# Grouped-query attention on one core: GpSimd's share of VectorE's exp product sized by the stretch beside which it runs

## The chip, the core and the metric

The kernel runs on one core of a Trainium2 chip. The core has TensorE (PE in the profile, its weight loads PEld), VectorE (DVE), ScalarE (ACT), GpSimd (POOL) and SyncE (SP); each takes its own instructions in order, and DMA queues move data beside them. The metric is the device time of one execution in microseconds (us); the kernel before takes 361.26 us, the median of three runs (361.14 to 361.68).

## What is computed

For 8 batches, 8 query heads and 2 key/value heads, 1024 positions and head size 64, in float32:

```
scores = q @ k.T / sqrt(64)          # 1024 x 1024 for each of the 64 (batch, head)
attn   = exp(scores - max) ; attn = attn / (sum(attn) + 1e-8)
out    = attn @ v                    # query heads 0-3 use key/value head 0, heads 4-7 head 1
```

The kernel leaves out the maximum (the inputs are small) and divides by the sum at the very end, after the product with the values, to which a column of ones is added so that the same matmul gives the sum.

## The kernel before

A "head" below is one of the 64 pairs (batch, query head). The 1024 keys of a head are eight blocks of 128. For one block, TensorE makes the scores with all 1024 queries in one of three PSUM slots `sp0` to `sp2` (two matmuls of 64x512 columns, line 794). Then one of two engines takes the exponential of the 128x1024 scores out of PSUM:

- ScalarE by one ACTIVATE into a buffer `pt` (line 804).
- VectorE by a "chain". One TENSOR_SCALAR from PSUM (`dpass`, line 815) turns the scores into 16-bit numbers `yt` whose bits are exponent and fraction. When two blocks are there, three operations on 128x2048 elements in SBUF follow: `zh` (line 822) makes a second factor from the fraction's bits in `zt`, `two` (line 829) takes the power of two into `et`, and `mul` (line 838) multiplies `yt` into `zt`. The sum of `et` and `zt` is the exponential; TensorE adds them by using both as weights. Only in the last three heads (TAIL) does VectorE add them itself (`add`, line 843).

In the steady part GpSimd takes a part of each `mul`: the last 320 of the 1024 columns of each block of a chain (`GC`, line 57; line 768), so VectorE multiplies 2 x 704 columns. At most two products wait for GpSimd at a time (`GQ`); a chain that finds them waiting multiplies all 2048 columns on VectorE. Which of the blocks go to VectorE is set by a quota: two of the eight blocks of every head, three in every tenth head (`MXD`, `MORE`).

The second matmuls (`pv`, line 856) use blocks of exp as weights and the values as the moving operand, 65 columns each, and fill banks `op0` and `op1` with seven 65-column pieces at a time. When a bank is full VectorE makes seven reciprocals (`rec`, line 921) and multiplies (`norm`, line 930) out of PSUM into `ost`; SyncE's queue stores a head's result (line 934).

GpSimd's queue holds, in one order: the products (line 768), the copies of values into `va`, a tile for all 16 (batch, key/value head) (`place_v`, line 596), and the DMA issues that cast queries and keys to bf16 in DRAM (`cast_q`, `cast_k`, lines 563 to 582). SyncE's queue holds the loads that turn them (lines 604 and 614), copies of the keys, loads of values and the stores.

The order of every queue is written before the kernel is built by a planner (class `Plan`). It keeps a clock for TensorE, ScalarE and VectorE with a duration for each instruction (the `M_` constants), lets ScalarE take its blocks in turn, lets VectorE take, in this order, a waiting `dpass`, a `rec`, or the best of a `norm` and the chains' next steps (`dve`, lines 201 to 277), and at each choice of TensorE tries the alternatives for `HORIZON` ns ahead and keeps the one with the least idle time of ScalarE (weight `W_A`), of VectorE (`W_D`) and lost time of TensorE (`W_P`). A product for GpSimd is put down at the start of a `dpass` (`gpsimd`, lines 188 to 199), so it runs beside it, and it waits for the VectorE instruction ahead of that `dpass` (line 771). PE work that uses a product is planned for `M_GLATE` ns after its end.

The cast DMAs have due times. After the first product each is held until a product is emitted whose successor is over 2300 ns off, and then stands behind that product in GpSimd's queue (lines 773 to 775); one held for over 3000 ns is emitted at the next event, wherever that is (lines 754 and 755). Each waits for the last score matmul emitted before it (line 751).

Of the kernel before, what the change touches and what calls it, by code (L numbers as in the profile page):

```python
# [20 lines left out]
M_SEE = 51  # L21
# [4 lines left out]
M_PVTAIL = 180  # L26
M_ACT = 917
M_ATAIL = 107
M_FIX = 66
# [5 lines left out]
M_REC = 90  # L35
M_GP = 850
M_GLATE = 1500

# [5 lines left out]

HORIZON = 5500
W_A = 1.0
W_D = .28
W_P = .1
W_LAG = 0
# [4 lines left out]
MXD = 2  # L54
MORE = 10
TAIL = 3
GC = 320
GQ = 2
STEPS = (("zh", M_D4), ("two", M_D4), ("mul", M_D2), ("add", M_D2))


class Chain:


    def __init__(self, id, nsteps):
        self.id, self.nsteps = id, nsteps
        self.pairs = []
        self.at = 0
        self.parts = 1
        self.cols = 1024  # L70
        self.end = 0
# [7 lines left out]
    def left(self):  # L79
        n = len(self.pairs)  # L80
        return sum(
            M_FIX + (self.cols if k == "mul" else 1024) * n * r
            for k, r in STEPS[self.at : self.nsteps]
        )


class State:
    LISTS = "nxt dcount pcnt pmax a_of mms slot aq dq out norms lastp firstp twice".split()

    def copy(self):  # L90
        c = State.__new__(State)
        c.__dict__.update(self.__dict__)
        for k in self.LISTS:
            setattr(c, k, getattr(self, k)[:])
        new = {}

        def twin(ch):
            if ch is None:
                return None
# [6 lines left out]
        c.gq = [(t, twin(x), i) for t, x, i in self.gq]  # L106
        c.heads = {k: v[:] for k, v in self.heads.items()}
        c.ev = None
        return c
# [6 lines left out]
class Plan:  # L116
# [5 lines left out]
    def __init__(self, nj, npt, nct, nyt):  # L122
# [7 lines left out]
        self.group_of = [g for g, (lo, hi) in enumerate(self.groups) for _ in range(lo, hi)]  # L130
        self.qready = [M_START] + [M_START + M_Q1 + M_QSTEP * j for j in range(nj - 1)]
        s = State()
        s.nxt = [0] * nj
# [7 lines left out]
        s.out = [M_START, M_START]  # L141
        s.norms, s.gq = [], []
        s.tP = s.tA = M_START
# [43 lines left out]

    def gpsimd(self, s, t, j):

        g = s.placed + 1  # L190
        if 4 * g - 1 <= j < self.nj and 4 * g < self.nj:
            s.placed = g
            s.note(t, "gplace", None, g, None)
            s.tG = t + M_GP
        elif s.gq and s.gq[0][0] <= t and s.tG <= t:
            _, ch, i = s.gq.pop(0)
            s.note(t, "gmul", None, ch.id, i)
            s.tG = t + M_GP
            self.part(s, ch, s.tG + M_SEE + M_GLATE)

    def dve(self, s):
        t, nj, end = s.tD, self.nj, None
        if s.dq and s.dq[0][0] <= t:
            _, sl, j, c = s.dq.pop(0)
# [9 lines left out]
            ch = s.open  # L214
            ch.pairs.append((j, c))
            if j not in s.heads[ch.id]:
                s.heads[ch.id].append(j)
            self.gpsimd(s, t, j)
            s.note(t, "dpass", sl, (ch.id, len(ch.pairs) - 1), (j, c))
            end = t + M_FIX + 1024 * M_D1  # L220
            s.slot[sl] = end + M_DTAIL + M_SEE
            s.dlast = (ch.id, 0)
            if len(ch.pairs) == 2:
                s.chains.append(ch)
                s.open = None
        elif s.norms and s.norms[0][0] <= t and s.norms[0][1] == "rec":
            _, _, lo, hi = s.norms[0]
            s.note(t, "rec", (lo, hi), None, None)
            end = t + M_REC
            s.dlast = lo  # L230
            s.norms[0] = (end, "norm", lo, hi)
        else:
            best = None
            if s.norms and s.norms[0][0] <= t:
                late = s.dlast == s.norms[0][2]
                best = (late, 5 if late else 0, None)
            for ch in s.chains:

                late = s.dlast == (ch.id, ch.at) and ch.at in (0, 3)
                key = (late, 3 - ch.at, ch)  # L240
                if best is None or key[:2] < best[:2]:
                    best = key
            if best:
                at = max(t, s.dend + M_DEP) if best[0] else t
                ch = best[2]
                if ch is None:
                    _, _, lo, hi = s.norms.pop(0)
                    s.note(t, "norm", (lo, hi), None, None)
                    end = at + M_FIX + 64 * (hi - lo) * M_D1
                    s.out[self.group_of[lo] % 2] = end + M_DTAIL + M_SEE  # L250
                    s.dlast = None
                    s.end = s.pc == self.last and not s.left and not s.norms
                else:
                    n = len(ch.pairs)
                    kind, rate = STEPS[ch.at]
                    if kind == "zh" and GC and ch.pairs[0][0] < nj - 5 and len(s.gq) < GQ:
                        end = at + M_FIX + 1024 * n * rate
                        s.gq += [(end + M_DTAIL + M_SEE, ch, i) for i in range(n)]
                        ch.parts += n
                        ch.cols -= GC  # L260
                    cols = ch.cols if kind == "mul" else 1024
                    s.note(t, kind, None, ch.id, n, cols)
                    end = at + M_FIX + cols * n * rate
                    ch.at += 1
                    s.dlast = (ch.id, ch.at)
                    if ch.at == ch.nsteps:
                        s.chains.remove(ch)
                        self.part(s, ch, end + M_DTAIL + M_SEE)
# [4 lines left out]
        else:  # L273
            s.tD = max(t, s.tP) + 1
            for q in (s.dq, s.norms):
                if q:
                    s.tD = min(s.tD, q[0][0])

    def pick_d(self, s):
        for j in range(s.a, min(self.nj, s.a + 3)):  # L280
            if s.nxt[j] < 8 and s.dcount[j] < MXD + (j % MORE == MORE // 2) and self.qready[j] <= s.tP:
                return j
        return None

    def choices(self, s):
# [14 lines left out]
        dj = None  # L300
        held = len({ch.id for ch in s.chains} | {x[1].id for x in s.gq})
        if not s.dq and held < self.nyt and (s.open or s.used_c < self.nct):
# [184 lines left out]
def kernel(  # L487
# [29 lines left out]
    NCT = 8  # L517
    NYT = 4
    plan = Plan(NJ, NPT - 2, NCT - 1, NYT - 1)

# [39 lines left out]
    nc.vector.memset(va[:, :, :, :, D : D + 1], 1.0)  # L560
    kt, qt, qd, kd, vs = {}, {}, {}, {}, {}
# [33 lines left out]
    def place_v(b, g):  # L595
        return nc.gpsimd.tensor_copy(  # L596
            out=va[:, b * G + g, :, :, 0:D],
            in_=vs.pop((b, g)).rearrange("p c (two d) -> p c two d", two=2),
# [130 lines left out]
    def flat(t):  # L729
        return t.bitcast(BF16).rearrange("p i a b -> p i (a b)")  # L730

# [21 lines left out]
    for when, kind, x, j, c, *cols in ev:  # L753
        if casts and casts[0][0] < when - 3000:
            cast(*casts.pop(0)[1:])
        if kind in ("ck", "cq"):

            if gps is None or not GC:
                cast(kind, j)
            else:  # L760
                casts.append((when, kind, j))
        elif kind in ("gmul", "gplace"):
# [3 lines left out]
            else:  # L766
                z = flat(zt[j])[:, c, 1024 - GC :]
                gps = nc.gpsimd.tensor_tensor(  # L768
                    out=z, in0=flat(yt[j])[:, c, 1024 - GC :], in1=z, op=ALU.mult
                )  # L770
# [39 lines left out]
        elif kind == "dpass":  # L810
            ch, i = j
            where[c] = j
            if i == 0:
                yt[ch] = yp.tile([128, 2, 2, HS], U16, name="yt")
            vec = nc.vector.tensor_scalar(  # L815
# [3 lines left out]
        elif kind == "zh":  # L819

            zt[j] = zp.tile([128, 2, 2, HS], U16, name="zt")
            vec = nc.vector.tensor_scalar(  # L822
# [3 lines left out]
        elif kind == "two":  # L826

            et[j] = ep.tile([128, 2, 2, HS], U16, name="et")
            vec = ins = nc.vector.tensor_scalar(  # L829
# [6 lines left out]
        elif kind == "mul":  # L836
            z = flat(zt[j])[:, 0:c, 0 : cols[0]]
            vec = nc.vector.tensor_tensor(  # L838
                out=z, in0=flat(yt[j])[:, 0:c, 0 : cols[0]], in1=z, op=ALU.mult
            )  # L840
# [5 lines left out]
        elif kind == "pv":  # L846
# [7 lines left out]
            for i in range(j, j + c):  # L854
# [10 lines left out]
        elif kind == "pvf":  # L865
# [4 lines left out]
            for i in range(NPIECE):  # L870
# [4 lines left out]
                for n, p in enumerate(every):  # L875
                    nc.tensor.matmul(
                        ops[i // 4][:, lo : lo + D + 1],
                        lhsT=p[:, i // 2 * 128 : (i // 2 + 1) * 128],
                        rhs=va[:, 0, ci % NH, ci // NH, :],
                        start=(first and i % 4 == 0 and n == 0),  # L880
# [3 lines left out]
        elif kind == "pvl":  # L884
# [4 lines left out]
            for i in range(NPIECE):  # L889
# [5 lines left out]
                for n, (ci, p) in enumerate(every):  # L895
                    nc.tensor.matmul(  # L896
                        sps[plan.spare][:, i // 4, lo : lo + D + 1],
                        lhsT=p[:, i // 2 * 128 : (i // 2 + 1) * 128],
                        rhs=va[:, b * G + h // HPG, ci % NH, ci // NH, :],
                        start=(first and i % 4 == 0 and n == 0),  # L900
# [68 lines left out]
```

The softmax here doesn't subtract the row's maximum and nothing guards it: scores larger than these inputs give would overflow.

## Time and profile before

| | us |
|---|---|
| median of three runs | 361.26 |
| lowest and highest | 361.14, 361.68 |
| span of the profiled execution | 359.6 |
| PE busy | 348.5 (97%) |
| DVE busy | 349.7 (97%), 494 instructions |
| ACT busy | 351.1 (98%), 382 instructions, 378 of them exponentials |
| POOL busy | 124.6 (35%) |

The profiled execution's own time is its span; the median of the runs is 1.6 us above it. In the profile a group's line reads: line of the code, engine, operation, output and inputs with their shapes, the number of instructions, then busy time, mean duration of one in ns, and the idle time just before them with what ended it. In the view of instructions in order of time a line starts with the start and the duration in us. An ACT or DVE record ends a little after the next instruction has started, since results are still being written, so durations add up to more than the busy time.

### The profile page before, as it was taken

Reading aid. Unit: us, or ns where it says so; the run is one execution under the profiler, and the core shown is the slowest. Engines: PE = TensorE matmul, PEld = TensorE weight load, DVE = VectorE, ACT = ScalarE, POOL = GpSimd, SP = SyncE. Lnnn points to the kernel's source line nnn. Section 1 sums busy time; section 2 is a strip of 40 time slices with the busy share of each in tenths; the row PEclk is TensorE's granted clock in tenths of the full one; section 3 lists DMA queues with packets and bytes.
Section 4 is the critical chain, followed back from the end, with each engine's and each line's share of the span. In section 5 each row is a group of like instructions: output and inputs, shape, how many; then the busy total and the mean of one; then the engine's idle time right before and its main releaser. Section 6 shows DMA issues by size and latency. Waiting matters only on the chain.

```text
span 359.6 us, 14110 instructions
## 1 busy us (share of the span) xinstructions
PE 348.5 (97%) x6223; PEld 224.1 (62%) x6223; DVE 349.7 (97%) x494; ACT 351.1 (98%) x382; POOL 124.6 (35%) x190
## 2 busy tenths in 40 slices
PE   8889999999999999999999999999999999999995
PEld 4446666666666666666666666666666566666664
DVE  4999999999999999999999999999999999999994
ACT  5999999999999999999999999999999999999995
POOL 4134244344443344242333534144414243321000
PEclk9999999999999999999999999999999999999999
DMA  8634675664697868567557877666477457655132
GB/s 186 114 52 115 138 120 137 132 121 119 132 161 119 148 117 152 113 111 164 120 102 143 128 163 125 132 126 140 107 114 163 105 118 132 154 129 106 46 89 89
DMA packets 89404, 44.82 MB, mean 125 GB/s; under 512 B 46000, under 2 KB 87600, under 8 KB 88112
## 3 DMA queue, kind: packets, MB, share of 16 engines
q1 hardware_dynamic: 86208, 33.44, 41.5%
q0 software_dynamic: 2992, 10.23, 20.4%
q8 instruction: 48, 0.79, 0.9%
q10 hardware_dynamic: 144, 0.26, 0.2%
q14 instruction: 12, 0.10, 0.1%
HBM read 25.17 MB, written 27.00 MB: 145 GB/s over the span
## 4 chain that ended last, share of the span: by engine, by line
DVE 71%; ACT 19%; PE 4%; issue 4%; DMA 1%; DVEq 0%
DVE yt L815 34%; ACT pt L804 19%; DVE zt L838 12%; DVE et L829 8%; DVE ost L930 7%; DVE zt L822 7%; DVE rec L921 2%; PE ops L856 2%; PE sp L794 2%; DMA q<-in_q_dram 1%; PE sp L896 1%; PE sp L673 0%; DVE kt L694 0%; PE ops L685 0%; ACT q L662 0%
## 5 line engine op out<-in xcount | busy, mean ns | idle before, releaser
L804 ACT ACTIVATE pt<-sp 128x1024 bf16<-128x1024 f32 x378 | 348.5, 1051 | 0.7 <-PE sp L794 0.5
L794 PE MATMUL sp<-qt,kt 64*128 64x512 bf16 x1024 | 173.4, 382 | 5.8 <-ACT pt L804 2.7
L856 PE MATMUL ops<-va,pt 128*128 128x65 bf16 x2928 | 176.0, 194 | 0.0
L815 DVE TENSOR_SCALAR yt<-sp 128x1024 uint16<-128x1024 f32 x134 | 162.5, 1213 | 0.5 <-PE sp L794 0.5
L856 PEld LDWEIGHTS <-pt 128*128 128x128 bf16 x2928 | 130.9, 97 | 32.9 <-issue 32.9
L856 PE MATMUL ops<-va,zt 128*128 128x65 bf16 x1040 | 125.7, 194 | 0.0
L856 PE MATMUL ops<-va,et 128*128 128x65 bf16 x1008 | 119.5, 194 | 0.0
L768 POOL TENSOR_TENSOR zt<-yt,zt 128x320 bf16<-128x320 bf16 x90 | 71.0, 789 | 120.1 <-DVE zt L838 32.9
L856 PEld LDWEIGHTS <-et 128*128 128x128 bf16 x1008 | 81.2, 98 | 21.3 <-issue 21.0
L856 PEld LDWEIGHTS <-zt 128*128 128x128 bf16 x1040 | 84.8, 97 | 10.2 <-issue 10.2
L794 PEld LDWEIGHTS <-kt 64*128 64x128 bf16 x1024 | 49.0, 93 | 58.2 <-issue 37.0
L838 DVE TENSOR_TENSOR zt<-yt,zt 128x1408 bf16<-128x1408 bf16 (+1 forms) x67 | 66.2, 989 | 0.0
L571 POOL DMA_DIRECT2D qd<-in_q_dram x62 | 36.0, 581 | 45.0 <-PE sp L794 41.8
L822 DVE TENSOR_SCALAR zt<-yt 128x2048 uint16<-128x2048 uint16 x67 | 46.2, 689 | 0.4
L829 DVE TENSOR_SCALAR et<-yt 128x2048 uint16<-128x2048 uint16 x67 | 45.4, 677 | 0.0
L930 DVE TENSOR_TENSOR ost<-ops,rec 128x448 f32<-128x448 f32 (+2 forms) x73 | 44.4, 608 | 0.4
L596 POOL CAST va<-vs 128x512 bf16<-128x512 f32 x16 | 9.8, 614 | 24.1 <-DVE ost L930 8.8
L921 DVE RECIPROCAL rec<-ops 128x7 f32<-128x7 f32 (+2 forms) x73 | 14.0, 192 | 0.0
L579 POOL DMA_DIRECT2D kd<-in_k_dram x15 | 8.5, 569 | 11.6 <-PE sp L794 11.6
L650 PE MATMUL ops<-warm 128*128 128x128 bf16 (+1 forms) x63 | 9.2, 265 | 1.2 <-DVE warm L559 1.2
L650 PEld LDWEIGHTS <-warm 128*128 128x128 bf16 x63 | 4.4, 104 | 6.7 <-issue 5.5
L843 DVE TENSOR_TENSOR zt<-et,zt 128x2048 bf16<-128x2048 bf16 x3 | 3.7, 1221 | 0.0
(37 smaller groups left out, 24.4 us busy)
## 6 DMA issues: line engine op xcount, KB each, us to landing
out_dram<-ost SPq DMA_DIRECT2D x64, 256.0 KB, 3.1
qd<-in_q_dram POOLq DMA_DIRECT2D x63, 128.0 KB, 3.5
vs<-in_v_dram SPq DMA_DIRECT2D x16, 256.0 KB, 3.3
kd<-in_k_dram POOLq DMA_DIRECT2D x15, 128.0 KB, 3.1
kt<-kt SPq DMA_DIRECT2D x30, 64.0 KB, 2.9
qt<-qd SPq DMA_TRANSPOSE x63, 4.0
q<-in_q_dram ACTq DMA_DIRECT2D x1, 256.0 KB, 3.2
kt<-kd SPq DMA_TRANSPOSE x15, 3.8
```

The lines of the kernel that those rows point to most:

```text
L571: return nc.gpsimd.dma_start(out=t.rearrange("(a x) d -> a (x d)", x=4), in_=q[b, h].rearrange("(a x) d -> a (x d)", x=8),)
L650: nc.tensor.matmul(ops[bank][:, lo : lo + cols], lhsT=warm[:, 0:128], rhs=warm[:, 0:cols], start=not beside, stop=True, skip_group_check=b ...
L768: gps = nc.gpsimd.tensor_tensor(out=z, in0=flat(yt[j])[:, c, 1024 - GC :], in1=z, op=ALU.mult)
L794: now = nc.tensor.matmul(sps[x][:, half, :], lhsT=t[lo : lo + D, c // NH, ci % NH * 128 : (ci % NH + 1) * 128], rhs=qt[j][lo : lo + D, 0, ...
L804: exps.append(nc.scalar.activation(out=p, in_=where_s[(j, c)], func=AF.Exp, scale=scale))
L815: vec = nc.vector.tensor_scalar(out=yt[ch][:, i, :, :], in0=where_s[c], scalar1=EXP_A, scalar2=EXP_B, op0=ALU.mult, op1=ALU.add,)
L822: vec = nc.vector.tensor_scalar(out=zt[j][:, 0:c], in0=yt[j][:, 0:c], scalar1=0x7F, scalar2=0x3F00, op0=ALU.bitwise_and, op1=ALU.bitwise_or,)
L829: vec = ins = nc.vector.tensor_scalar(out=et[j][:, 0:c], in0=yt[j][:, 0:c], scalar1=0x7F80, scalar2=None, op0=ALU.bitwise_and,)
L838: vec = nc.vector.tensor_tensor(out=z, in0=flat(yt[j])[:, 0:c, 0 : cols[0]], in1=z, op=ALU.mult)
L856: nc.tensor.matmul(ops[plan.group_of[x] % 2][:, lo : lo + D + 1], lhsT=p[:, qs * 128 : (qs + 1) * 128], rhs=va[:, b * G + h // HPG, ci % N ...
L921: vec = nc.vector.reciprocal(out=to, in_=sums)
L930: vec = nc.vector.tensor_tensor(out=to, in0=o, in1=by, op=ALU.mult)
```

## The change

The products for GpSimd are no longer a fixed 320 columns of each block. At the start of a `dpass` the planner looks at the stretch in which VectorE will read PSUM: the `dpass` alone (1134 ns), or with a `norm` behind it (531 ns more), or with a `rec` ahead and a `norm` behind. From that it takes away a lead and a fixed cost and divides the rest by 2.09 ns per column; so many columns, in steps of 32, are taken off the end of the two blocks of a chain, seen as 2048 columns in a row. A chain waits with its `mul` for up to two such products (`GWINS`), and VectorE may stay idle for up to 500 ns for a coming `dpass` rather than start that `mul` (`M_SPARE`). When a `norm` is ready it is put right behind the next `dpass` (`follow`). Chains that begin in the first two heads or the last five get no product.

The quota of VectorE is two blocks of a head and three in every fifth head, and 2, 1, 1 in the first three. `va` is four tiles in a ring. Chains' buffers `yt` are six, not four. The planner's ScalarE duration is 923 ns, not 917, `HORIZON` 8000, not 5500, and `W_P` 0; the order of all queues is a new plan.

The instructions of the two kernels, by count: exponentials on ScalarE 378 and 374; `dpass` 134 and 138; `zh` and `two` 67 each and 70 each (two of them of 1024 elements); `mul` 67 (45 of 1408 columns and 22 of 2048) and 70 (21 of 960, 13 of 2048, 13 of 1632, 9 of 1216, 5 each of 1376 and 1248, 2 of 1024, one of 928 and one of 1344); `add` 3, and 3 and one of 1024; products on GpSimd 90 of 320 columns, and 58 of 416, 26 of 672, 5 of 384 and 2 of 704; `rec` and `norm` 74 each in both; the DMAs are the same.

```diff
-M_ACT = 917
+M_ACT = 923
...
-M_GP = 850
-M_GLATE = 1500
+M_GP = 800
+M_GLEAD = 160
+M_GFIX = 120
+M_GCOL = 2.09
+M_GOVER = 60
+M_GLATE = 900
+M_NORM = 531
+M_HOLD = 2500
+M_SPARE = 500
...
-HORIZON = 5500
+HORIZON = 8000
...
-W_P = .1
+W_P = 0
...
-MORE = 10
+MORE = 5
 TAIL = 3
-GC = 320
-GQ = 2
+CHN = 2
+LONG = 6
+FIRST = (2, 1, 1)
+GWINS = 2
+GFROM = 2
+GTO = 5
+GMIN = 192
+GSTEP = 32
...
-        self.cols = 1024
+        self.cols = 0
+        self.wins = 0
+        self.zend = INF
...
+        self.quota = [FIRST[j] if j < len(FIRST) else MXD + (j % MORE == MORE // 2) for j in range(nj)]
...
-    def gpsimd(self, s, t, j):
-
+    def gpsimd(self, s, t, j, window):
+
+
+        at = max(t, s.tG)
+        until = t + window + M_GOVER
+        at += M_GLEAD
         g = s.placed + 1
-        if 4 * g - 1 <= j < self.nj and 4 * g < self.nj:
+        if 4 * g - 1 <= j < self.nj and 4 * g < self.nj and at + 614 <= until:
             s.placed = g
             s.note(t, "gplace", None, g, None)
-            s.tG = t + M_GP
-        elif s.gq and s.gq[0][0] <= t and s.tG <= t:
-            _, ch, i = s.gq.pop(0)
-            s.note(t, "gmul", None, ch.id, i)
-            s.tG = t + M_GP
+            at = s.tG = at + 614
+        for ch in s.chains:
+            if not (ch.zend <= at and 1 <= ch.at <= 2 and ch.nsteps == 3):
+                continue
+            if not GFROM <= ch.pairs[0][0] < self.nj - GTO:
+                continue
+            w = int((until - at - M_GFIX) / M_GCOL) // GSTEP * GSTEP
+            if w < GMIN:
+                break
+            if ch.cols - w < GMIN:
+                w = ch.cols
+            if not w:
+                continue
+            ch.cols -= w
+            ch.wins += 1
+            s.note(t, "gmul", None, ch.id, (ch.cols, w))
+            s.tG = at = at + M_GFIX + w * M_GCOL
+            ch.parts += 1
             self.part(s, ch, s.tG + M_SEE + M_GLATE)
+            break
...
     def dve(self, s):
         t, nj, end = s.tD, self.nj, None
-        if s.dq and s.dq[0][0] <= t:
+        norm = s.norms and s.norms[0][0] <= t
+        rec = norm and s.norms[0][1] == "rec"
+        soon = s.dq and s.dq[0][0] <= t + (M_REC if rec else 0)
+        if rec:
+            _, _, lo, hi = s.norms[0]
+            if soon:
+                self.gpsimd(s, t, s.dq[0][2], M_REC + 1134 + M_NORM)
+                s.host = True
+            s.note(t, "rec", (lo, hi), None, None)
+            end = t + M_REC
+            s.dlast = lo
+            s.norms[0] = (end, "norm", lo, hi)
+        elif s.dq and s.dq[0][0] <= t and not (norm and t - s.norms[0][0] > M_HOLD):
...
+            ch.cols += 1024
             if j not in s.heads[ch.id]:
                 s.heads[ch.id].append(j)
-            self.gpsimd(s, t, j)
+            if not s.host:
+                self.gpsimd(s, t, j, 1134 + (M_NORM if norm else 0))
+            s.host = False
+            s.follow = bool(norm)
...
             best = None
-            if s.norms and s.norms[0][0] <= t:
+            if norm:
                 late = s.dlast == s.norms[0][2]
-                best = (late, 5 if late else 0, None)
+                key = -1 if s.follow or s.norms[0][2] < NPIECE else 5 if late or s.dq else 0
+                best = (late and key >= 0, key, None)
             for ch in s.chains:
 
                 late = s.dlast == (ch.id, ch.at) and ch.at in (0, 3)
-                key = (late, 3 - ch.at, ch)
+                first = (3, 4, 2, 1)[ch.at]
+                if ch.at == 2 and ch.nsteps == 3 and ch.cols and ch.wins < GWINS:
+                    if GFROM <= ch.pairs[0][0] < nj - GTO:
+                        if s.dq and s.dq[0][0] < t + M_SPARE:
+                            continue
+                        first = 6
+                key = (late, first, ch)
                 if best is None or key[:2] < best[:2]:
                     best = key
+            s.follow = False
...
                     kind, rate = STEPS[ch.at]
-                    if kind == "zh" and GC and ch.pairs[0][0] < nj - 5 and len(s.gq) < GQ:
-                        end = at + M_FIX + 1024 * n * rate
-                        s.gq += [(end + M_DTAIL + M_SEE, ch, i) for i in range(n)]
-                        ch.parts += n
-                        ch.cols -= GC
-                    cols = ch.cols if kind == "mul" else 1024
-                    s.note(t, kind, None, ch.id, n, cols)
-                    end = at + M_FIX + cols * n * rate
+                    cols = ch.cols if kind == "mul" else 1024 * n
+                    end = at
+                    if cols:
+                        s.note(t, kind, None, ch.id, n, cols)
+                        end = at + M_FIX + cols * rate
+                    if kind == "zh":
+                        ch.zend = end + M_DTAIL + M_SEE
...
-    NYT = 4
-    plan = Plan(NJ, NPT - 2, NCT - 1, NYT - 1)
+    NYT = 6
+    NVA = 4
+    plan = Plan(NJ, NPT - 2, NCT - 1, NYT - 2)
...
-    va = kvp.tile([128, B * G, NH, 2, D + 1], BF16, name="va")
+    va = [kvp.tile([128, NH, 2, D + 1], BF16, name=f"va{i}") for i in range(NVA)]
...
-                z = flat(zt[j])[:, c, 1024 - GC :]
+                lo, w = c
+                z = flat(zt[j])[:, lo : lo + w]
                 gps = nc.gpsimd.tensor_tensor(
-                    out=z, in0=flat(yt[j])[:, c, 1024 - GC :], in1=z, op=ALU.mult
+                    out=z, in0=flat(yt[j])[:, lo : lo + w], in1=z, op=ALU.mult
                 )
...
-                    rhs=va[:, b * G + h // HPG, ci % NH, ci // NH, :],
+                    rhs=va[(b * G + h // HPG) % NVA][:, ci % NH, ci // NH, :],
```

More of the change, by code (lines that the diff above doesn't have):

```diff
@@ L81, in left, with share @@
         return sum(
-            M_FIX + (self.cols if k == "mul" else 1024) * n * r
+            M_FIX + (self.share() if k == "mul" else 1024 * n) * r
             for k, r in STEPS[self.at : self.nsteps]
         )
+    def share(self):
+        return max(0, self.cols - 500 * max(0, GWINS - self.wins)) if self.nsteps == 3 else self.cols
 class State:
@@ L105, in copy @@
         c.open = twin(self.open)
-        c.gq = [(t, twin(x), i) for t, x, i in self.gq]
         c.heads = {k: v[:] for k, v in self.heads.items()}
@@ L141, in __init__ @@
         s.out = [M_START, M_START]
-        s.norms, s.gq = [], []
+        s.norms = []
+        s.host = s.follow = False
         s.tP = s.tA = M_START
@@ L222, in dve @@
             s.dlast = (ch.id, 0)
-            if len(ch.pairs) == 2:
+            if len(ch.pairs) == (2 if j < LONG or j >= nj - 6 else CHN):
                 s.chains.append(ch)
                 s.open = None
[L226 to L231, printed above, removed]
         else:
             best = None
-            if s.norms and s.norms[0][0] <= t:
+            if norm:
                 late = s.dlast == s.norms[0][2]
-                best = (late, 5 if late else 0, None)
+                key = -1 if s.follow or s.norms[0][2] < NPIECE else 5 if late or s.dq else 0
+                best = (late and key >= 0, key, None)
             for ch in s.chains:
                 late = s.dlast == (ch.id, ch.at) and ch.at in (0, 3)
-                key = (late, 3 - ch.at, ch)
+                first = (3, 4, 2, 1)[ch.at]
[5 more added lines that the diff above has]
+                key = (late, first, ch)
                 if best is None or key[:2] < best[:2]:
                     best = key
+            s.follow = False
             if best:
@@ L277, in dve @@
                     s.tD = min(s.tD, q[0][0])
+            s.tD = max(s.tD, t + 1)
     def pick_d(self, s):
         for j in range(s.a, min(self.nj, s.a + 3)):
-            if s.nxt[j] < 8 and s.dcount[j] < MXD + (j % MORE == MORE // 2) and self.qready[j] <= s.tP:
+            if s.nxt[j] < 8 and s.dcount[j] < self.quota[j] and self.qready[j] <= s.tP:
                 return j
@@ L300, in choices @@
         dj = None
-        held = len({ch.id for ch in s.chains} | {x[1].id for x in s.gq})
+        held = len(s.chains)
         if not s.dq and held < self.nyt and (s.open or s.used_c < self.nct):
@@ L559 @@
     nc.vector.memset(warm, 0.0)
-    nc.vector.memset(va[:, :, :, :, D : D + 1], 1.0)
+    for t in va:
+        nc.vector.memset(t[:, :, :, D : D + 1], 1.0)
     kt, qt, qd, kd, vs = {}, {}, {}, {}, {}
@@ L596, in place_v @@
         return nc.gpsimd.tensor_copy(
-            out=va[:, b * G + g, :, :, 0:D],
+            out=va[(b * G + g) % NVA][:, :, :, 0:D],
             in_=vs.pop((b, g)).rearrange("p c (two d) -> p c two d", two=2),
@@ L729, in flat @@
     def flat(t):
-        return t.bitcast(BF16).rearrange("p i a b -> p i (a b)")
+        return t.bitcast(BF16).rearrange("p i a b -> p (i a b)")
     def terms(j, par, only=range(NC)):
@@ L756 @@
         if kind in ("ck", "cq"):
-            if gps is None or not GC:
+            if gps is None:
                 cast(kind, j)
@@ L813 @@
             if i == 0:
-                yt[ch] = yp.tile([128, 2, 2, HS], U16, name="yt")
+                yt[ch] = yp.tile([128, CHN, 2, HS], U16, name="yt")
             vec = nc.vector.tensor_scalar(
@@ L819 @@
         elif kind == "zh":
-            zt[j] = zp.tile([128, 2, 2, HS], U16, name="zt")
+            zt[j] = zp.tile([128, CHN, 2, HS], U16, name="zt")
             vec = nc.vector.tensor_scalar(
@@ L826 @@
         elif kind == "two":
-            et[j] = ep.tile([128, 2, 2, HS], U16, name="et")
+            et[j] = ep.tile([128, CHN, 2, HS], U16, name="et")
             vec = ins = nc.vector.tensor_scalar(
@@ L836 @@
         elif kind == "mul":
-            z = flat(zt[j])[:, 0:c, 0 : cols[0]]
+            z = flat(zt[j])[:, 0 : cols[0]]
             vec = nc.vector.tensor_tensor(
-                out=z, in0=flat(yt[j])[:, 0:c, 0 : cols[0]], in1=z, op=ALU.mult
+                out=z, in0=flat(yt[j])[:, 0 : cols[0]], in1=z, op=ALU.mult
             )
@@ L878 @@
                         lhsT=p[:, i // 2 * 128 : (i // 2 + 1) * 128],
-                        rhs=va[:, 0, ci % NH, ci // NH, :],
+                        rhs=va[0][:, ci % NH, ci // NH, :],
                         start=(first and i % 4 == 0 and n == 0),
@@ L898 @@
                         lhsT=p[:, i // 2 * 128 : (i // 2 + 1) * 128],
-                        rhs=va[:, b * G + h // HPG, ci % NH, ci // NH, :],
+                        rhs=va[(b * G + h // HPG) % NVA][:, ci % NH, ci // NH, :],
                         start=(first and i % 4 == 0 and n == 0),
```

## The prediction

> **What bounds the kernel now.** I read the page's busy times first, then the chain that ended last, the groups of instructions with each shape apart, and the instructions in order of time at the start, at the end, and where GpSimd works.
>
> ```profile
> span 359.6 us, 14110 instructions
> PE 348.5 (97%) x6223; PEld 224.1 (62%) x6223; DVE 349.7 (97%) x494; ACT 351.1 (98%) x382; POOL 124.6 (35%) x190
> DVE 71%; ACT 19%; PE 4%; issue 4%; DMA 1%; DVEq 0%
> ```
>
> VectorE and ScalarE are busy to the same per cent, and the chain changes between them. TensorE's 97% is no third bound: its matmuls overlap (a score matmul is recorded at 382 ns, yet six of them fit into 1.31 us), and the list of waits has TensorE wait only 2.7 us for ScalarE and 0.4 us for VectorE.
>
> ```profile
> 6.29 14.77 ACT L804 ACTIVATE pt<-sp 128x1024 bf16<-128x1024 f32 x16 [0.32 <-PE sp L794]
> 337.54 17.64 ACT L804 ACTIVATE pt<-sp 128x1024 bf16<-128x1024 f32 x19
> ...
> 8.28 1.23 DVE L815 TENSOR_SCALAR yt<-sp 128x1024 uint16<-128x1024 f32 x1 [0.48 <-PE sp L794]
> 355.70 0.21 DVE L921 RECIPROCAL rec<-sp 128x8 f32<-128x8 f32 x1 [1.47 <-PE sp L896]
> ```
>
> ScalarE's exponentials run from 6.29 to 337.54 + 17.64 = 355.18 us, 348.9 us for 378, 0.922 each, with no gap. VectorE goes from 6.58 us with one wait of 0.48 at the start and one of 1.47 before its last reciprocal. So both are full: a gain needs less work on both.
>
> ```profile
> L804 ACT ACTIVATE pt<-sp 128x1024 bf16<-128x1024 f32 x378 | 348.5, 1051 | 0.7 <-PE sp L794 0.5
> L815 DVE TENSOR_SCALAR yt<-sp 128x1024 uint16<-128x1024 f32 x134 | 162.5, 1213 | 0.5 <-PE sp L794 0.5
> L768 POOL TENSOR_TENSOR zt<-yt,zt 128x320 bf16<-128x320 bf16 x90 | 71.0, 789 | 120.1 <-DVE zt L838 32.9 <-DVE ost L930 31.0 <-DVE et L829 29.4
> L822 DVE TENSOR_SCALAR zt<-yt 128x2048 uint16<-128x2048 uint16 x67 | 46.2, 689 | 0.4
> L829 DVE TENSOR_SCALAR et<-yt 128x2048 uint16<-128x2048 uint16 x67 | 45.4, 677 | 0.0
> L930 DVE TENSOR_TENSOR ost<-ops,rec 128x448 f32<-128x448 f32 x70 | 43.0, 614 | 0.3
> L838 DVE TENSOR_TENSOR zt<-yt,zt 128x1408 bf16<-128x1408 bf16 x45 | 39.8, 885 | 0.0
> L838 DVE TENSOR_TENSOR zt<-yt,zt 128x2048 bf16<-128x2048 bf16 x22 | 26.4, 1200 | 0.0
> ```
>
> These are the durations. A VectorE record's last 0.08 us lies under the next (a `dpass` at 150.87 lasts 1.22, the next starts at 152.00), so I use the mean less 0.08. One more view shows the price of GpSimd work that is in the way:
>
> ```profile
> 85.18 1.22 DVE L815 TENSOR_SCALAR yt<-sp 128x1024 uint16<-128x1024 f32 x1
> 86.31 0.90 DVE L829 TENSOR_SCALAR et<-yt 128x2048 uint16<-128x2048 uint16 x1
> ...
> 85.28 0.55 POOL L571 DMA_DIRECT2D qd<-in_q_dram  x1 [1.20 <-PE sp L794]
> 85.85 0.80 POOL L768 TENSOR_TENSOR zt<-yt,zt 128x320 bf16<-128x320 bf16 x1
> ```
>
> A product normally starts 0.16 to 0.24 us after its `dpass` and ends before it. Here a cast issue stood ahead of it in GpSimd's queue, so it started 0.67 us after, ended at 86.65, 0.34 into `two`, and `two` took 0.90 instead of 0.68. The stall, 0.22, is the overlap less 0.12. At 51.18 the overlap is 0.47, `mul` takes 1.23 instead of 0.88, and the same difference remains. The first 0.12 us of overlap is thus free.
>
> **The change part by part.**
>
> ScalarE: 374 exponentials for 378, -4 x 0.922 = -3.7 us.
>
> VectorE's work. Four more `dpass`, 4 x 1.133 = +4.5. `zh` and `two`: one more full pair, 0.61 + 0.60, and two pairs of half size, estimated at 0.33 an operation, +2.5 together. One more `add` of half size, +0.6 (half of the 1.12 of a full product). The `mul`: the 1408- and 2048-column rows give (1.120 - 0.805)/640 = 0.5 ns a column and some 0.1 us fixed; with the nearer fit of 0.521 and 0.067, the 70 new ones with 96,384 columns come to 54.8, the old to 45 x 0.805 + 22 x 1.120 = 60.9: -6.1. Sum +1.6.
>
> VectorE's own order. A `zh` right behind the `dpass` that it needs starts 1.25 us after it instead of 1.13, and a `norm` right behind its `rec` 0.22 instead of 0.11. In the order of instructions the first stands 13 times before and 9 times after, the second 13 and 8: 9 x 0.11 = -1.0. VectorE's own sum is +0.6.
>
> Products that come late. Before, 12 of the 90 start over 0.1 us later than usual, all behind a cast issue, by 0.35 on average; 320 columns leave 1.13 - 0.20 - 0.79 + 0.12 = 0.26 us free, and only six stalls result, 0.35, 0.22, 0.16, 0.15, 0.15 and 0.09 = 1.1 us. The new products have 416 or 672 columns. Only 320 have a row (0.789). Bounds for a column are 0.614/512 = 1.2 ns (the value copy's 512 columns in 0.614) and 0.789/320 = 2.46 (nothing fixed). From 320 they give 0.90 to 1.03 for 416 and 1.21 to 1.66 for 672. Near 2.1 ns, to which a product with its two inputs is nearer than the copy, I take 0.99 and 1.52. Such a product alone ends 0.02 to 0.10 past its stretch (1.133, or 1.133 + 0.534 with `norm`): inside the free 0.12. But the spare falls from 0.26 to 0.06, and 0.17 for the 24 products with a `rec` behind the `dpass`, 0.10 in the mean. An overdue cast stands directly ahead of a product 27 times before and 22 after; at 12 in 27 that is 10 late ones, each charged 0.35 - 0.10: 2.5 us, +1.4 on before. Bounds: none late, -1.1; all 22, 5.5 - 1.1 = +4.4. I take +1.4, since casts are still emitted by the same rule.
>
> The rule that speaks against this change is in the Trainium skill, SBUF — State Buffer, section Who interferes with whom: GpSimd and a VectorE operation that needs the shared port pair exclude each other for the whole instruction, "not throttle". Read without the free 0.12, it would charge 67 products 0.06 each, +4 us; the rows of `two` and `mul` above show the free part, so it stays out.
>
> Cast issues on time. Some end inside a `zh` or `two` and hold it (at 89.18 `zh` takes 0.75); such places cost 0.6 us in all. Behind a longer product the issue starts when the next `zh` is already running; at 134.67 an issue with `zh` soon behind it lost and stretched to 1.05 while `zh` took its 0.69. Bounds 0 and -0.6, taken -0.4.
>
> A `norm` beside a product: 33 of the new products lie beside one. No row shows it beyond 8 ns. Bounds: nothing, or a wait to the product's end, 0.20 + 1.52 - 1.13 - 0.12 = 0.47, x 33 = 15.5 us. `dpass` and `rec`, which also read PSUM, run beside products at their usual durations, so I take nothing. The same section of the skill says that an operation with at most one SBUF input outside the two-port modes does not contend; no run here shows it for `norm`.
>
> Idle time. VectorE's two waits, 0.5 and 1.5, are the places that could shrink, since ScalarE now has 3.7 us to spare at the end; against it the planner may now hold a `mul` and idle up to 0.5 us for a host. Bounds -1.5 and +3 (six such waits), taken -0.5.
>
> The ring of values (16 copies of 0.61 in both, their reader four groups on), the four small memsets (VectorE waits 2.2 us for the first load there), six `yt` buffers and 4 x 8 fewer ScalarE weights, replaced by twice as many from VectorE (TensorE has room between matmuls), cost nothing; if GpSimd's lateness exceeded the planned 0.9 us, TensorE would wait in order and both engines after it.
>
> The sum on VectorE: +0.6 + 1.4 - 0.4 - 0.5 = +1.1 us; 359.6 becomes 360.7. The median stands 1.6 above the profiled span, so 362.4. ScalarE alone would allow 3.7 less: VectorE becomes the bound.
>
> **The rivals.**
>
> Faster: products are hardly ever late, as the new plan puts casts elsewhere. Then +0.6 - 1.1 - 0.6 - 0.5 = -1.6, 359.7; with the last wait gone too 358.7; ScalarE's floor is 361.3 - 3.7 = 357.6. For: only 22 casts, not 27, directly ahead. Against: the spare of 0.06. It decides from five late products or fewer. Chance 0.30.
>
> No change: half of the late price, or VectorE's last wait absorbs it: 360.6 to 361.9. Chance 0.18.
>
> Slower through longer products: at 2.46 ns a column 672 take 1.66 and end 0.07 past the free part; 33 x 0.07 = 2.3, and late ones 0.1 more, 1.0: 365.7. Against: some fixed cost is likely, as the copy has. Chance 0.10.
>
> Slower through `norm` blocked: +15.5, 377.9. For: nothing but the missing row. Chance 0.04.
>
> **How the numbers follow.** My forecast (362.0 to 364.0) has 0.38. Slower by over 0.2% (0.7 us, about what this kernel's measurement can tell from no change) is 0.38 + 0.10 + 0.04 = 0.52. The range 358.8 to 365.5 leaves out the lower half of faster and the `norm` case.
>
> **What would show it.** ScalarE with gaps of 4 us or more in sum and VectorE with hardly any would show VectorE as the bound. Products of 416 at 0.99 and 672 at 1.52 would show the sizes right; `norm` beside them at 0.61, that it isn't blocked. Late products should stand behind casts, and the `zh`, `two` or `mul` behind them be longer by the overlap less 0.12. I am wrong if VectorE has gaps of several us, if ScalarE is still without any, or if late products are few.

## The result and the profile after

The changed kernel takes 361.88 us (median of 20 runs, 361.42 to 362.47), the kernel before 361.32 (20 runs, 360.89 to 361.77): 1.0016 of it, 95% interval 1.0010 to 1.0023. GpSimd does half as much again of the product, VectorE and ScalarE are arranged anew, and it ends 0.16% later, less than the 0.2% that the prediction takes for a change. The profiled execution has a span of 360.1 us, before 359.6.

From the page of the kernel after, busy times and the chain that ended last:

```profile
span 360.1 us, 14126 instructions
PE 349.0 (97%) x6214; PEld 222.7 (62%) x6214; DVE 350.8 (97%) x511; ACT 349.3 (97%) x378; POOL 156.0 (43%) x191
DVE 65%; PE 30%; issue 4%; DVEq 0%
```

ScalarE has left the chain (the last line gives each engine's share of it). VectorE has gained 1.1 us of busy time and GpSimd 31. The chain's 30% of TensorE looks like a new bound; the experiments speak against that.

Instructions in order of time at both ends of the kernel after (start, duration, in brackets the idle time ahead and what ended it):

```profile
6.33 4.69 ACT L863 ACTIVATE pt<-sp 128x1024 bf16<-128x1024 f32 x5 [0.62 <-PE sp L853]
334.87 19.38 ACT L863 ACTIVATE pt<-sp 128x1024 bf16<-128x1024 f32 x21
...
6.75 1.22 DVE L874 TENSOR_SCALAR yt<-sp 128x1024 uint16<-128x1024 f32 x1 [0.27 <-PE sp L853]
8.46 1.23 DVE L874 TENSOR_SCALAR yt<-sp 128x1024 uint16<-128x1024 f32 x1 [0.48 <-PE sp L853]
355.66 0.21 DVE L980 RECIPROCAL rec<-sp 128x8 f32<-128x8 f32 x1 [0.58 <-PE sp L955]
355.90 0.69 DVE L989 TENSOR_TENSOR ost<-sp,rec 128x512 f32<-128x512 f32 x1
```

ScalarE ends its 374 exponentials at 354.25, only 0.9 us earlier than before with 3.7 us less to do: 347.9 us, 0.930 each. VectorE has 0.75 us of waits at the start and 0.58 before the last reciprocal (1.47 before), and between them the list of waits has none. Its last instruction ends at 356.59; before, it started at 355.94 and lasted 0.69, to 356.63. So VectorE's end did not move. The span's 0.4 us come after it: 3.46 us from there to the end, 3.01 before. ScalarE's visible gaps come to 1.8 us in the row below, not to the 4 that the prediction named as a sign; the rest of its slower pace lies beneath its records.

Groups with each shape apart (busy, mean ns of one, idle ahead), kernel after:

```profile
L863 ACT ACTIVATE pt<-sp 128x1024 bf16<-128x1024 f32 x374 | 346.7, 1034 | 1.8 <-PE sp L853 1.1
L881 DVE TENSOR_SCALAR zt<-yt 128x2048 uint16<-128x2048 uint16 x68 | 46.0, 677 | 0.3
L888 DVE TENSOR_SCALAR et<-yt 128x2048 uint16<-128x2048 uint16 x68 | 45.6, 672 | 0.0
L989 DVE TENSOR_TENSOR ost<-ops,rec 128x448 f32<-128x448 f32 x70 | 42.9, 613 | 0.1
L827 POOL TENSOR_TENSOR zt<-yt,zt 128x416 bf16<-128x416 bf16 x58 | 56.4, 972 | 61.4 <-DVE et L888 24.3 <-DVE zt L881 23.5 <-DVE ost L989 6.7
L827 POOL TENSOR_TENSOR zt<-yt,zt 128x672 bf16<-128x672 bf16 x26 | 37.8, 1453 | 37.6 <-DVE zt L881 22.6 <-DVE et L888 13.6 <-DVE zt L897 1.4
L827 POOL TENSOR_TENSOR zt<-yt,zt 128x384 bf16<-128x384 bf16 x5 | 4.6, 917 | 0.1
```

A product of 416 columns takes 0.972 us and one of 672 takes 1.453: 1.88 ns a column and 0.19 us fixed. `norm`, beside 33 of them, takes 613 ns as it did (614).

Counted from the start of each VectorE instruction to the next, against its kind's usual time, nine places lose time to a product: 2.5 us, before six and 1.1. Five of the nine have a late cast issue ahead of the product, as predicted (1.25 us), and one, with a product that is not late, loses 0.02. The other three (1.22 us) look alike, GpSimd first and then VectorE:

```profile
317.55 0.61 POOL L654 CAST va<-vs 128x512 bf16<-128x512 f32 x1 [0.75 <-DVE et L888]
318.10 0.55 POOL L629 DMA_DIRECT2D qd<-in_q_dram  x1
318.67 0.92 POOL L827 TENSOR_TENSOR zt<-yt,zt 128x384 bf16<-128x384 bf16 x1
...
317.41 1.21 DVE L874 TENSOR_SCALAR yt<-sp 128x1024 uint16<-128x1024 f32 x1
318.54 0.61 DVE L989 TENSOR_TENSOR ost<-ops,rec 128x448 f32<-128x448 f32 x1
319.07 1.20 DVE L897 TENSOR_TENSOR zt<-yt,zt 128x1248 bf16<-128x1248 bf16 x1
```

In this stretch the planner put a value copy and then a product of 384 columns, 0.61 + 0.92, which fit. Between them stands a cast issue of 0.55, which no one planned. The product ends at 319.59, 0.52 into the `mul`, and that takes 1.20 us where it should take 0.80. The code asks whether the next product is over 2300 ns off, but looks only at planned times later than the present one; copy and product of one stretch have the same time, so the product is not seen.

### The profile page after: what moved, and what is told of

It reads as the page before. It is cut to its first block, busy times and chain, and to the rows that moved or that the text cites. A ratio compares the mean times of both kernels' runs of the same rounds, so it can differ in the third digit from the quotient of the medians.

```text
span 360.1 us, 14126 instructions
## 1 busy us (share of the span) xinstructions
PE 349.0 (97%) x6214; PEld 222.7 (62%) x6214; DVE 350.8 (97%) x511; ACT 349.3 (97%) x378; POOL 156.0 (43%) x191
## 4 chain that ended last, share of the span: by engine, by line
DVE 65%; PE 30%; issue 4%; DVEq 0%
DVE yt L874 32%; PE ops L915 15%; PE sp L853 13%; DVE zt L897 11%; DVE et L888 7%; DVE ost L989 7%; DVE zt L881 6%; DVE rec L980 2%; PE ops L708 1%; DVE zt L902 1%; PE sp L955 1%; PE sp L731 0%; PE ops L743 0%; PE ops L731 0%; DVE warm L616 0%
## 5 line engine op out<-in xcount | busy, mean ns | idle before, releaser
L874 DVE TENSOR_SCALAR yt<-sp 128x1024 uint16<-128x1024 f32 x138 | 167.3, 1212 | 0.8 <-PE sp L853 0.8
L915 PEld LDWEIGHTS <-pt 128*128 128x128 bf16 x2896 | 128.4, 97 | 37.8 <-issue 37.8
L827 POOL TENSOR_TENSOR zt<-yt,zt 128x416 bf16<-128x416 bf16 (+3 forms) x91 | 101.8, 1118 | 101.8 <-DVE zt L881 47.5
L897 DVE TENSOR_TENSOR zt<-yt,zt 128x960 bf16<-128x960 bf16 (+6 forms) x70 | 62.0, 887 | 0.0
L708 PE MATMUL ops<-warm 128*128 128x128 bf16 (+1 forms) x30 | 5.2, 311 | 1.7 <-DVE warm L616 1.2
L708 PEld LDWEIGHTS <-warm 128*128 128x128 bf16 x30 | 2.4, 111 | 5.1 <-issue 4.0
L902 DVE TENSOR_TENSOR zt<-et,zt 128x2048 bf16<-128x2048 bf16 (+1 forms) x4 | 4.3, 1072 | 0.0
```

Source lines behind the costliest of these rows:

```text
L708: nc.tensor.matmul(ops[bank][:, lo : lo + cols], lhsT=warm[:, 0:128], rhs=warm[:, 0:cols], start=not beside, stop=True, skip_group_check=b ...
L827: gps = nc.gpsimd.tensor_tensor(out=z, in0=flat(yt[j])[:, lo : lo + w], in1=z, op=ALU.mult)
L874: vec = nc.vector.tensor_scalar(out=yt[ch][:, i, :, :], in0=where_s[c], scalar1=EXP_A, scalar2=EXP_B, op0=ALU.mult, op1=ALU.add,)
L897: vec = nc.vector.tensor_tensor(out=z, in0=flat(yt[j])[:, 0 : cols[0]], in1=z, op=ALU.mult)
L915: nc.tensor.matmul(ops[plan.group_of[x] % 2][:, lo : lo + D + 1], lhsT=p[:, qs * 128 : (qs + 1) * 128], rhs=va[(b * G + h // HPG) % NVA][: ...
```

## The experiments

The theory: VectorE is the bound, and each of its stalls lies on the path. The rival: TensorE's order (30% of the chain) or the new plan's rhythm holds both engines, and a stall only takes the place of a wait.

**No cast between a copy and a product of one stretch** (e1_place).

```diff
     casts = []
+    met = []
...
             later = [t for t in begun if t > when]
-            if casts and (not later or later[0] > when + 2300):
+            met.append(when)
+            if casts and begun.count(when) == met.count(when) and (not later or later[0] > when + 2300):
```

> The changed kernel, but no cast issue is put between a value copy and the product of the same stretch; plan and every VectorE, ScalarE and TensorE instruction stay. In its profile three of the nine stalls of VectorE, 0.41 us each, stand behind such a trio (copy, issue, product of 384 columns). Theory (VectorE is the bound and each stall lies on the path): these three stalls vanish and the time falls by about 1.2 us, to 360.7. Rival (TensorE's order, which makes up 30% of the chain that ended last, holds both engines, so a VectorE stall only takes the place of a wait): less than 0.4 us.

Measured: 361.05 us, 0.9990 of before (0.9982 to 0.9999), so 0.8 us less than the changed kernel. The same place in its profile:

```profile
316.93 0.61 POOL L654 CAST va<-vs 128x512 bf16<-128x512 f32 x1 [0.75 <-DVE et L890]
317.50 0.91 POOL L828 TENSOR_TENSOR zt<-yt,zt 128x384 bf16<-128x384 bf16 x1
318.36 0.55 POOL L629 DMA_DIRECT2D qd<-in_q_dram  x1
...
318.45 0.80 DVE L899 TENSOR_TENSOR zt<-yt,zt 128x1248 bf16<-128x1248 bf16 x1
```

The `mul` takes 0.80, the stalls' sum falls to 1.27, and the span by 1.0 to 359.1. That is less than the theory's 1.2, and at least twice the most that the rival allows: 0.8 by the medians, 0.9 by the ratios to the kernel before, 1.0 in the profiles.

**No overdue cast right ahead of a product either** (e3_both).

```diff
-        if casts and casts[0][0] < when - 3000:
+        near = any(when <= t < when + 1300 for t in begun)
+        if casts and casts[0][0] < when - 3000 and not near:
```

> As e1_place, and an overdue cast is not emitted while a product or copy is due within 1300 ns, so none stands right ahead of a late product. Theory: all nine stalls (2.5 us in sum) go, the time falls by 2.0 to 2.5 us, to 359.4 to 359.9, under the kernel before. Rival: TensorE's order holds, 361.4 or more. A third: the casts come later by up to 1.2 us and a query load then waits, a gap of TensorE before a score.

Measured: 359.70 us, 0.9954 (0.9942 to 0.9967). The stalls fall to 0.14 us and the time by 2.2, as the theory has it: with TensorE's instructions in the same order, removing 2.35 us from VectorE removed 2.2 from the kernel's median. The profiled span fell by 1.6 only, since VectorE has a new wait of 0.71 us in it. TensorE's share of the chain was no bound. The third possibility showed too, though not from the later casts:

```profile
9.56 0.69 DVE L884 TENSOR_SCALAR zt<-yt 128x2048 uint16<-128x2048 uint16 x1
10.97 1.22 DVE L877 TENSOR_SCALAR yt<-sp 128x1024 uint16<-128x1024 f32 x1 [0.71 <-PE sp L856]
...
10.54 0.60 PE L856 MATMUL sp<-qt,kt 64*128 64x512 bf16 x4 [0.85 <-DMA qt<-qd]
```

TensorE waits for the second head's queries, whose cast is issued before any of the held ones. In the profile of the changed kernel the same instructions come without that wait. So whether TensorE waits at the start of this plan depends on when that load lands, and in this profile it costs VectorE 0.7 us.

**The size of the products alone undone** (e4_cap320).

```diff
-            w = int((until - at - M_GFIX) / M_GCOL) // GSTEP * GSTEP
+            w = min(320, int((until - at - M_GFIX) / M_GCOL) // GSTEP * GSTEP)
```

> The changed kernel with no product wider than 320 columns, as before the change, and everything else of the change kept (the planner makes 108 such products, 137 dpasses, 375 exponentials). GpSimd takes 34,560 columns instead of 44,928. Theory (VectorE is the bound): +10,368 x 0.52 = 5.4 us of mul, -2.4 for one dpass less with its steps and its add, -1.5 for stalls that 320 columns leave room for: +1.5 us, 363.4. Rival (the new plan, not the sizes, sets the time): within 0.5 us of 361.9.

Measured: 362.63 us, 1.0030 (1.0019 to 1.0042), slower than the changed kernel by 0.75 us in the medians and by 0.5 in the ratios. The sign is the theory's and the size at most half of it; the run does not decide between the theory and the rival's "within 0.5". The stalls stayed at 1.27 us, three of them again behind a cast put between copy and product, and VectorE had a wait of 0.97 for the load at the start. In the profiles VectorE ends at 356.94, only 0.35 us later than in the changed kernel; the other 0.51 of the span comes after it, where two stores are issued instead of one and 3.97 us follow instead of 3.46. So what the sizes alone are worth on VectorE is not shown; in this plan it is less than 1 us.

**The cast rule on the kernel before** (e5_before_overdue). The edit is the `near` line above, on the kernel before.

> The kernel before with the rule of e3_both for overdue casts alone: none is emitted while a product is due within 1300 ns. In its profile six stalls of VectorE, 1.1 us in sum, stand behind such casts. Theory (ScalarE has no gap there from 6.3 to 355.2 us and is as full as VectorE): the stalls go, VectorE gets gaps or a longer wait at the end, and the time falls by no more than 0.3 us, 361.0 to 361.3. Rival (VectorE alone sets the time before): -1.1 us, 360.2.

Measured: 360.41 us, 0.9968 (0.9956 to 0.9981): -0.9 us. Here my theory falls. VectorE's wait at the end is what it was, and ScalarE became faster:

```profile
6.31 2.85 ACT L805 ACTIVATE pt<-sp 128x1024 bf16<-128x1024 f32 x3 [0.45 <-PE sp L795]
339.30 14.82 ACT L805 ACTIVATE pt<-sp 128x1024 bf16<-128x1024 f32 x16
...
354.63 0.21 DVE L922 RECIPROCAL rec<-sp 128x8 f32<-128x8 f32 x1 [1.46 <-PE sp L897]
```

Its 378 exponentials take 347.8 us, not 348.9. Hardly a gap of ScalarE showed before (0.7 us), and yet 1.1 us of its run were waits that could go: a record lasts 1.05 us and the next starts about 0.92 after it, so a wait under some 0.1 us lies beneath the record before. Counted from start to start, 38 exponentials before are followed after more than 0.95 us, with 3.4 us above 0.922, here 32 with 2.2.

This run allows a comparison that the changed kernel itself does not: with the casts out of the products' way in both, the new arrangement takes 359.70 us against 360.41, 0.7 less in the medians and 0.5 in the ratios, whose intervals overlap (0.9942 to 0.9967 and 0.9956 to 0.9981).

**GpSimd's queue made longer at the start** (e6_pad), where it has nothing to do:

```diff
+    pad = kvp.tile([128, 1], FP32, name="pad")
...
         elif kind == "pl":
             place_v(*j)
+            for _ in range(16):
+                nc.gpsimd.memset(pad, 0.0)
```

> The changed kernel with 16 memsets of one column into an unused tile added to GpSimd's queue near the start, where it has nothing to do; nothing else is moved. In the profile of the changed kernel, and of the two with its plan run since, the time from the end of VectorE's last instruction to the end of the span is 3.44 to 3.46 us, in the kernel before 3.01; 0.3 of it lies between GpSimd's last semaphore and its drain (0.37 against 0.08). Theory (the place in GpSimd's own instruction stream at which the program ends makes the difference, as with a block of instructions that has to be loaded): with 16 more instructions ahead, that gap is 0.08 again and the time falls by about 0.4 us, to 361.5. Rival (the queues' last stores or the plan make it): 3.4 us and 361.9 as before.

Measured: 361.58 us, 1.0006 (0.9997 to 1.0015). Its span is 360.3 us, VectorE's last instruction starts at 356.64 and lasts 0.69: 3.0 us to the end, as before the change. The drains of GpSimd's queue, of the kernel before, the changed one and this one (number, then shortest, median and longest ns):

```profile
L964 POOLq DRAIN  x3: 39/102/7475, 329.2 to 359.4; - x3
```

```profile
L1023 POOLq DRAIN  x3: 39/250/7276, 328.6 to 359.8; - x3
```

```profile
L1026 POOLq DRAIN  x3: 39/93/7272, 329.3 to 360.1; - x3
```

The drain of middle length, in the program's last microsecond, takes 250 ns in the changed kernel and about 100 in the others, and starts 0.3 us later too. That 16 idle instructions far ahead take this away is shown here and by the next run; that a block of instructions has to be loaded there is only my guess. In the times it is 0.3 us with overlapping intervals, in part because VectorE ended 0.7 us later here, behind the wait for the load (0.65).

**Both cast rules and the 16 memsets** (e9_both_pad).

> The kernel of e3_both with the 16 memsets of e6_pad. Theory: the same 0.4 us, 359.3. Rival: 359.7.

Measured: 359.47 us, 0.9947 (0.9934 to 0.9961), against 0.9954 without them; 3.0 us after VectorE's end, not 3.4. The difference in time, 0.2, is inside the intervals; the profile shows it.

**The planner's cost of a product as measured** (e7_refit).

```diff
-M_GFIX = 120
-M_GCOL = 2.09
+M_GFIX = 177
+M_GCOL = 1.9
```

> The kernel of e3_both with the products' cost in the planner as the profile of the changed kernel has it (320, 416 and 672 columns at 0.789, 0.972 and 1.451 us: 177 ns and 1.9 ns a column in place of 120 and 2.09). The stretches then hold 448 and 704 columns; GpSimd takes 47,616 columns, VectorE 2,688 fewer. Theory (VectorE is the bound and a product may end 0.12 us past its stretch): -2,688 x 0.52 = -1.4 us, 358.3. Rival (the new plan's waits take it back, or ScalarE is the bound by now): 359.4 to 360.2.

Measured: 360.46 us, 0.9972 (0.9961 to 0.9983), 0.8 slower than with the old constants. The theory is out, and the time lies above the rival's range too. The profiled execution tells less: 54 products of 448 columns, hardly a stall (0.1 us), VectorE's end at 354.56 against 355.02, a last wait of 1.07 for 0.64, and a drain that is slow at another place. The runs lie between 359.77 and 361.13. Why its median is higher stays open.

**VectorE's quota back**, `MORE = 10`, on the kernel with both cast rules (e8_quota10).

> The kernel of e3_both with VectorE's quota raised to three blocks in every tenth head only, as before the change: 132 dpasses, 380 exponentials, and GpSimd's products down to 30,304 columns since there are fewer stretches. VectorE has 6 x 1.13 + 3 x 1.21 less and 8,480 x 0.52 more, -6.0 us; ScalarE six exponentials more. It tells what ScalarE's own pace is, 0.922 us as its whole run had it, or the 0.905 to 0.912 at which most of its exponentials follow each other in the profile of the kernel before. Theory (0.922 holds hidden waits): ScalarE's run is 344 to 347 us and the time 357.5 to 360.0. Rival (0.922 is its own pace, so it was full before): 350.4 us, 362 to 363.

Measured: 365.08 us, 1.0101 (1.0087 to 1.0114). Both were wrong. VectorE has waits of 8.5 us and ScalarE takes 353.2 us for 380, 0.929 each, as slow as in the changed kernel (0.930) though VectorE has less to do. At the end VectorE waits for TensorE three times, 1.62, 0.87 and 2.53 us; the first is

```profile
348.90 0.21 DVE L983 RECIPROCAL rec<-ops 128x7 f32<-128x7 f32 x1 [1.62 <-PE ops L918]
```

So neither engine's work sets this time; that the order of the plan does is argued, not shown. ScalarE's own pace can't be had from this run.

**The second head's load later in the plan**, `M_Q1 = 5000`, once with the old (e10_pad_q1) and once with the measured cost of a product (e11_refit_pad_q1), both with the cast rules and the memsets.

> The kernel of e9_both_pad with the planner told that the queries of the second head are there 1.6 us later (5000 ns for 3400). In four of the five profiles of kernels with the changed plan and its quota since e3_both, TensorE waits 0.8 to 0.9 us at 9.7 us for that load and VectorE has a gap of 0.65 to 0.71 behind it; the profile of the changed kernel happens to have none. It is a new plan (GpSimd takes 47,008 columns, 2,080 more: -1.1 us of mul). Theory (VectorE is the bound from its first dpass on): the gap goes, 358.0 to 359.0. Rival (what VectorE loses less at the start it waits more at the end, or the new plan's waits take it): 359.3 to 360.

Measured: 360.21 us, 0.9961 (0.9948 to 0.9973). The expectation's "four of the five" includes the kernel of 320 columns, whose gap is 0.97. TensorE waits for the load no more, but VectorE has a wait of the same size instead, for the second matmuls:

```profile
13.35 0.18 DVE L986 RECIPROCAL rec<-ops 128x4 f32<-128x4 f32 x1 [0.82 <-PE ops L941]
```

Its last instruction starts at 352.99, 1.2 us earlier than in e9_both_pad, and ends at 353.69; the program ends 4.17 us after that, since the last store lands 3.21 us after VectorE's end, and 2.04 in e9_both_pad. The time is above the rival's range by 0.2 us, and by another way than the rival named: what VectorE won was lost behind it.

> The kernel of e7_refit with the 16 memsets and the later second head. GpSimd takes 48,832 columns, 1,824 more than in e10_pad_q1, -0.95 us of mul. Theory: 357.5 to 358.5. Rival (the wider products' gain is lost in waits, as in e7_refit, which ended later than e3_both): no faster than e10_pad_q1.

Measured: 358.70 us, 0.9929 (0.9913 to 0.9944), the fastest here: 0.7% under the kernel before, 0.9% under the changed one. It is 0.2 us above the theory's range, and the rival is out. From its profile:

```profile
L830 POOL TENSOR_TENSOR zt<-yt,zt 128x448 bf16<-128x448 bf16 x59 | 60.9, 1032 | 77.7 <-DVE zt L887 29.7 <-DVE et L894 26.4 <-DVE ost L995 13.8
L830 POOL TENSOR_TENSOR zt<-yt,zt 128x704 bf16<-128x704 bf16 x28 | 42.4, 1515 | 39.4 <-DVE et L894 20.4 <-DVE zt L887 16.2 <-DVE zt L903 2.8
352.90 0.21 DVE L986 RECIPROCAL rec<-sp 128x8 f32<-128x8 f32 x1 [1.21 <-PE sp L961]
353.14 0.69 DVE L995 TENSOR_TENSOR ost<-sp,rec 128x512 f32<-128x512 f32 x1
```

No VectorE instruction is held by a product, VectorE's end is 2.8 us before that of the changed kernel, and 3.0 us follow. The wait for the second matmuls near the start is there too, 0.78 us. The measured costs, which lost 0.8 us in one plan, are part of the fastest in another: single plans differ by about 1 us for reasons that these runs don't take apart.

## Why the prediction was right, and where not

The forecast was 362.4 us; it is 361.9. The direction held, and so did the mechanism on VectorE, but by 0.16% the case that came is the one I called "no change" and gave 0.18, not the slower one with 0.52. Term by term, on VectorE, in the profiled executions:

- *VectorE's work, +1.6.* The instructions' usual times sum to 343.35 before and 344.96 after: +1.6.
- *VectorE's own order, -1.0.* `zh` behind its `dpass` and `norm` behind its `rec` lost 2.94 us before, 1.92 after: -1.0.
- *Products that come late, +1.4.* 1.12 before and 2.49 after: +1.4, and e3_both shows that it lies on the path. The size is right partly by chance. I charged ten products behind overdue casts with 0.25 each; five came, 1.25 together, and three stood behind a cast in a stretch shared with a value copy, 1.22 together, which the order of GpSimd's queue would have shown.
- *Length of a product.* I took 0.99 and 1.52; they take 0.972 and 1.453.
- *Free overlap.* Products reach up to about 0.1 us past their stretch and nothing stalls, as the two rows of before had it. The rule of the Trainium skill, SBUF — State Buffer, Who interferes with whom, that the pair is exclusive for the whole instruction, is right about the rest of the overlap: at 319.07 the product runs 0.52 into the `mul`, which takes 0.40 longer. Charged from the record's start, the 50 products that end inside a `zh`, `two` or `mul` would have cost 4.8 us, the sum of their overlaps; 2.5 were lost.
- *`norm` beside a product, nothing.* 613 ns. The same section's sentence on operations with one SBUF input agrees with it.
- *Cast issues on time, -0.4.* 0.6 us of VectorE before by the usual durations of `zh` and `two`, none after: the bound, not the part of it that I took.
- *Idle time, -0.5.* The last wait fell from 1.47 to 0.58, and VectorE's first `dpass` comes 0.17 later, behind a wait of 0.27: -0.7.
- Not in the sum: an operation right behind a `rec` (a `zh`, `two`, `mul` or, more rarely, a `dpass`) is often about 0.04 us shorter than usual, 40 times before and 52 after: -0.5.

The sum predicted +1.1; VectorE's end moved by -0.04. What was missed comes to -0.9 of that: cast issues -0.2, steps behind `rec` -0.5, idle time -0.2; the last 0.2 us are within what counting by usual durations can resolve. What made the kernel slower all the same was in no step: the end of the program, +0.44 us, which 16 idle instructions remove, and possibly the wait for the load at the start, which the profile of the changed kernel escaped and others with its plan did not. That the time still came within 0.5 us of the forecast is luck: the sum was 1.1 us too high on VectorE, and 0.4 us came where it had nothing.

The step that failed is the first reading, "both are full: a gain needs less work on both", with its floor "ScalarE alone would allow 3.7 less". e5_before_overdue gained 0.9 us with ScalarE's work unchanged and 1.1 us less of stalls on VectorE. ScalarE's 0.922 held hidden waits: it is 0.920 there, 0.930 at the changed kernel with 374, 0.923 at e11_refit_pad_q1, and in every profile here a quarter of the exponentials start within 0.904 us of the one ahead. What it would be without any wait stays open. So VectorE's stalls set the time before as well, and what I called "VectorE becomes the bound" was no change. The sum on VectorE alone was the right one to make.

Of the rivals, "faster: products are hardly ever late" gave 358.7 to 359.7; e3_both, where they are not late, is 359.7. Products longer than taken (0.972 and 1.453 us), and a blocked `norm` (613 ns), are out.

## What to carry to other kernels

When work is sized to fill a stretch beside another engine, everything else in the helper's queue becomes a collision: read that queue instruction by instruction, the DMA issues too, and ask of each what it stands ahead of. Here that was worth 2.2 us, more than the sizing that the change is about: by the kernel of 320 columns that is less than 1 us. An engine without a visible gap is not thereby full: where records overlap, compare its start-to-start pace in two kernels before calling it a bound.

## What was not expected of the hardware

- With one plan, the program's end took 3.44 to 3.46 us after VectorE's last instruction, and 3.0 with 16 more instructions in GpSimd's queue, in two pairs of kernels: a drain near the end took 227 to 250 or about 100 ns. In e10_pad_q1 it took 4.17 with short drains, because the last store took 1.2 us longer to land; why it did is open.
- In the kernel before, a cast issue on GpSimd that started up to 0.26 us ahead of a VectorE `zh` or `two` (once 0.28) lost and was stretched from 0.55 to 0.93 us or more; those that started earlier took 0.49 to 0.55 us (one 0.83), and the six that ended 0.24 us or more into the operation held it, by 0.05 to 0.09 us and the long one by 0.2. That took 0.6 us of VectorE; behind the longer products, nothing.
- In the changed kernel eight products ended 0.21 to 0.54 us into a VectorE `zh`, `two` or `mul`, and each of those operations was longer by the overlap less 0.12 us: 0.23 gave 0.11, 0.54 gave 0.42. Forty-two more ended up to 0.11 us into one, and nothing was lost but 0.02 us in one place.
